# Index scores in small portions, two-bank ReLUs and sign-made masks in the token phase of a two-layer hybrid trunk

## The chip, the core and the metric

One core of one Trainium2 chip runs the whole program. The metric is the device time of one execution in microseconds (us): the median of three runs, and beside it one execution taken by the hardware profiler, from which all rows come.

## What is computed

Two layers over 1024 tokens of width 1024, float32. Every layer has one input projection, a sparse attention branch, a gated delta-rule branch, gates, and an output projection. The part that the change touches most is the lightning indexer, which picks 256 keys for each query:

```python
raw = jnp.einsum('bqhd,bsd->bqhs', qib, k_idx)                 # 8 heads of 64
iscore = jnp.einsum('bqhs,bqh->bqs', jax.nn.relu(raw), wb)
iscore = jnp.where(causal[None], iscore, -jnp.inf)
_, sel = lax.top_k(iscore, topk)                               # topk = 256, ties to the lower index
...
y_a = dsa_attention(q_a, k_a, v_a, q_i, k_i, w_i) * jax.nn.silu(z_a)
...
x = x + (gates[0] * y_a + gates[1] * y_b) @ w_out[layer]
```

The kernel doesn't gather keys: it makes a mask for every block of 128 queries whose row has more than 256 causal keys (blocks t = 2 to 7, with n = 128(t+1) keys, 384 to 1024), and attention adds the mask to its logits.

## The kernel before

Matrix products run as three products of rounded halves (high by high, high by low, low by high), so one product of 128 x 1024 by 1024 x 512 is 24 matmuls of 512 columns. PSUM has eight banks of 512 float32 columns for each partition. A layer goes through these stages:

- **make_h**: normalise x and transpose it (`tr` tiles, L289).
- **Token phase** (`token_phase`): the index projections; then three chunks of q, k and v, each over 8 token tiles (`proj_tokens`, L368, 24 matmuls a tile into an `acc` bank, emptied by ScalarE's copy `stage`, L415); then four gates, each of four `proj_feat` calls (L391, 24 matmuls; ScalarE's tanh `th`, L673, and VectorE's `gate`, L674, empty the bank). The weights are cast by ScalarE (`w_hi`, L150) and their rests made by VectorE (`w_lo`, L151).
- **Beside it** runs a generator, `self.beside`, first `index_scores`, then `select`. `index_scores` does, for each block and each pair of heads, 64-row matmuls for two heads side by side into `wide` banks (L554), a ReLU on ScalarE (L556), and on VectorE the weighted sum into `scores` (L561, L563). `select` finds the 256th largest score of every row by a search over 31 bits: in each step VectorE counts for blocks 5 and 7 (L589) and ScalarE does it by the sum of a Sign for blocks 4, 3, 2 and 6 (L607). Two such searches (`SEL_STAGES`) are interleaved. At its end VectorE makes the masks (L652 to L658: equal, a running count, two combinations, a product), and SyncE's queue stores them.
- **Feature phase** (gates of the other branch, convolutions, the delta rule), **attention** (L1131 logits, L1133 mask and row maximum, L1136 exponential, L1154 transposes, L1163 values) and the output projection.

The order of the work is that in which the program writes it: every engine takes its own instructions in that order. `tick`, called behind every token tile and every `proj_feat`, is what mixes the second stream in: it takes steps of `self.beside` until their costs come to `SHARE` = 4. A score step costs 2n/1024, a step of the search 1.5, and what the last step overshoots is forgotten. So the scores are written in bursts of up to 36 rows of matmul pairs between two token tiles, 11 bursts a layer; within a burst nothing else stands on PE between a pair of heads and the next. There are four one-bank `wide` tiles. For n over 512 a pair of heads is done in two equal halves of n (2 x 320, 2 x 384, 2 x 448, 2 x 512), with a ReLU for each half and head. Gates use the two `acc` banks alone. In layer 0 the token phase lies at 77 to 364 us of the span, in layer 1 at 1372 to 1654 us; the feature phase follows.

Of the kernel before, what the change touches and what calls it, by code (L numbers as in the profile page):

```python
# [58 lines left out]
SHARE, SEL_COST = 4.0, 1.5  # L59
# [19 lines left out]
STEP_PAIRS, STEP_CHUNKS = 6, 7  # L79

# [16 lines left out]
class Trunk:  # L97
    def __init__(self, ctx, tc, args):
# [10 lines left out]
        self.beside = None  # L109
# [185 lines left out]
    def tick(self):  # L295

        left = SHARE
        while left > 0 and self.beside is not None:
            cost = next(self.beside, None)
            if cost is None:  # L300
                self.beside = None
            else:
                left -= cost
# [50 lines left out]
    def proj_tokens(self, weights, act, evac, t0=0, tag=lambda t: "acc", then=None):  # L354
# [8 lines left out]
        for t, k in order:  # L363
# [3 lines left out]
            for i, (a, b) in enumerate(((act[0], 0), (act[0], 1), (act[1], 0))):  # L367
                nc.tensor.matmul(acc[t][:, :n], a[:, k, ts], ws[k][b][:, :n], start=k == 0 and i == 0,  # L368
                                 stop=k == KT - 1 and i == 2)
# [14 lines left out]
    def proj_feat(self, ws, half, act, evac, tag="acc"):  # L384

        hs = slice(half * 512, half * 512 + 512)
        acc = self.bank(tag)
        for k in range(KT):
            cs = slice((k % 4) * P, (k % 4 + 1) * P)
            for i, (a, b) in enumerate(((0, 0), (0, 1), (1, 0))):  # L390
# [7 lines left out]
        self.tick()  # L398


    def token_phase(self, l, ip, ht, first):
# [31 lines left out]
        with tc.tile_pool(name="tok", bufs=1) as p, self.banks(wide=(1, 4)):  # L433
            self.decays(l, p, raw)
            scores = {t: p.tile([P, (t + 1) * P], F32, name=f"scores{t}") for t in SEL}
            select = interleave([self.select(p, i, scores, *st) for i, st in enumerate(SEL_STAGES)])
            self.beside = itertools.chain(self.index_scores(l, p, raw, scores), select)
# [3 lines left out]
            for f in range(GATES[0]):  # L441
                self.gate_a(l, ht, f)
# [54 lines left out]
    def index_scores(self, l, p, raw, scores):  # L497
# [42 lines left out]
        later = queries(t0)  # L540
        for t in SEL:
# [3 lines left out]
            parts = 1 if n <= 512 else 2  # L545
            w = n // parts
            for i in range(IDXH // 2):
                rel = [p.tile([P, S], F32, name="relu", bufs=3) for _ in range(2)]
                for o in range(0, n, w):
                    ps = [self.bank("wide") for _ in range(2)]  # L550
                    for j, (a, b) in enumerate(((qh, kh), (qh, kl), (ql, kh))):
                        for half in range(2):
                            rows = slice(IDXD * half, IDXD * half + IDXD)
                            nc.tensor.matmul(ps[half][:, :w], a[rows, i], b[rows, o:o + w], start=j == 0, stop=j == 2)  # L554
                    for half in range(2):
                        nc.scalar.activation(rel[half][:, o:o + w], ps[half][:, :w], AF.Relu)  # L556
# [10 lines left out]
                yield 2 * n / S  # L567
# [3 lines left out]
    def select(self, p, which, scores, on_dve, on_act):  # L571
# [63 lines left out]
        for i in range(nb):  # L635
# [6 lines left out]
        for i in range(nb):  # L642
# [628 lines left out]
```

## Time and profile before

| what | value |
|---|---|
| median of 3 runs (lowest, highest) | 2610.4 us (2606.67, 2615.41) |
| the profiled execution's own time | 2613.37 us |
| its span, first to last instruction | 2611.6 us |
| mean granted TensorE clock over the span | 0.993 |
| PE busy | 2542.9 us, 97% |
| VectorE (DVE) busy | 1897.7 us, 73% |
| ScalarE (ACT) busy | 1344.3 us, 51% |
| GpSimd (POOL) busy | 160.0 us, 6% |

PE is the matmuls and PEld the weight loads that run under them. Matmuls are pipelined: a matmul of 512 columns is listed with about 0.4 us, while the next starts 0.23 us later. Idle time before an instruction is put down to the work that ended it (`<-` and an engine, a name and a line). PEclk is the granted clock as a share of full speed, so 0.50 is the lower of TensorE's two levels (1.2 instead of 2.4 GHz).

### The profile page before, as it was taken

Reading aid. Unit: us, or ns where it says so; the run is one execution under the profiler, and the core shown is the slowest. Engines: PE = TensorE matmul, PEld = TensorE weight load, DVE = VectorE, ACT = ScalarE, POOL = GpSimd, SP = SyncE. Lnnn points to the kernel's source line nnn. Section 1 sums busy time; section 2 is a strip of 40 time slices with the busy share of each in tenths; the row PEclk is TensorE's granted clock in tenths of the full one; section 3 lists DMA queues with packets and bytes.
Section 4 is the critical chain, followed back from the end, with each engine's and each line's share of the span. In section 5 each row is a group of like instructions: output and inputs, shape, how many; then the busy total and the mean of one; then the engine's idle time right before and its main releaser. Section 6 shows DMA issues by size and latency. Waiting matters only on the chain. (4 is left out here: it accounts for less than half of the span.)

```text
span 2611.6 us, 42034 instructions
## 1 busy us (share of the span) xinstructions
PE 2542.9 (97%) x14858; PEld 2110.7 (81%) x14858; DVE 1897.7 (73%) x5086; ACT 1344.3 (51%) x3107; POOL 160.0 (6%) x428
## 2 busy tenths in 40 slices
PE   7999999999999999999999999999999999999998
PEld 7777778888888888898796777878888888878986
DVE  7578977777887773797366779877777787647965
ACT  5559824444444333697245796333444444338952
POOL 0124000000000000000002340000000000000000
PEclk9999999999999999999999999999999999999999
DMA  4112333233333323430521232333223333324223
GB/s 126 50 57 80 91 92 81 54 67 71 72 66 75 70 56 95 147 101 30 164 59 42 65 98 76 91 75 76 50 65 76 68 70 74 101 78 130 85 79 136
DMA packets 296439, 211.35 MB, mean 81 GB/s; under 512 B 72290, under 2 KB 253604, under 8 KB 296228
## 3 DMA queue, kind: packets, MB, share of 16 engines
q1 hardware_dynamic: 290116, 188.73, 26.9%
q0 software_dynamic: 6112, 19.93, 3.2%
q8 instruction: 117, 1.92, 0.3%
q14 instruction: 94, 0.77, 0.1%
HBM read 162.19 MB, written 46.40 MB: 80 GB/s over the span
## 5 line engine op out<-in xcount | busy, mean ns | idle before, releaser
L391 PE MATMUL acc<-hi_t,w_hi 128*128 128x512 f32 x1240 | 505.1, 407 | 8.2 <-DVE gate L674 8.2
L391 PE MATMUL acc<-lo_t,w_hi 128*128 128x512 f32 x1240 | 504.2, 407 | 0.0
L391 PE MATMUL acc<-hi_t,w_lo 128*128 128x512 f32 x1240 | 500.5, 404 | 0.0
L150 ACT CAST w_hi<-w_raw 128x512 fp32r<-128x512 f32 (+1 forms) x336 | 201.4, 602 | 314.2 <-PE acc L391 161.4
L151 DVE TENSOR_TENSOR w_lo<-w_raw,w_hi 128x512 fp32r<-128x512 f32 (+1 forms) x336 | 223.9, 670 | 136.0 <-ACT w_hi L150 117.1
L368 PE MATMUL acc<-w_hi,hi_t 128*128 128x512 f32 (+1 forms) x768 | 285.9, 373 | 9.6 <-ACT stage L415 7.0
L368 PE MATMUL acc<-w_lo,hi_t 128*128 128x512 f32 (+1 forms) x768 | 284.3, 370 | 3.8 <-DVE w_lo L151 3.8
L368 PE MATMUL acc<-w_hi,lo_t 128*128 128x512 f32 (+1 forms) x768 | 283.2, 369 | 0.0
L391 PEld LDWEIGHTS acc<-hi_t,w_hi 128*128 128x128 f32 x1240 | 234.5, 189 | 56.8 <-DVE gate L674 10.0
L391 PEld LDWEIGHTS acc<-hi_t,w_lo 128*128 128x128 f32 x1240 | 234.6, 189 | 47.7
L391 PEld LDWEIGHTS acc<-lo_t,w_hi 128*128 128x128 f32 x1240 | 234.6, 189 | 45.7
L607 ACT ACTIVATE t_junk<-scores,t_bits 128x640 f16<-128x640 f32 x248 | 198.9, 802 | 35.2 <-DVE t_bits L599 26.0
L391 PE MATMUL more<-hi_t,w_hi 128*128 128x512 f32 x488 | 199.1, 408 | 0.0
L391 PE MATMUL more<-lo_t,w_hi 128*128 128x512 f32 x488 | 198.9, 408 | 0.0
L391 PE MATMUL more<-hi_t,w_lo 128*128 128x512 f32 x488 | 197.4, 405 | 0.0
L368 PEld LDWEIGHTS acc<-w_hi,hi_t 128*128 128x128 f32 x768 | 145.9, 190 | 40.4 <-ACT stage L415 8.7
L368 PEld LDWEIGHTS acc<-w_lo,hi_t 128*128 128x128 f32 x768 | 146.3, 190 | 29.8 <-DVE w_lo L151 7.7
L368 PEld LDWEIGHTS acc<-w_hi,lo_t 128*128 128x128 f32 x768 | 146.1, 190 | 21.9
L589 DVE TENSOR_SCALAR_CACHE_REDUCE t_junk<-scores,t_bits 128x1024 f16<-128x1024 f32 (+4 forms) x136 | 153.4, 1128 | 4.3
L563 DVE SCALAR_TENSOR_TENSOR scores<-relu,w_idx,scores 128x384 f32<-128x384 f32 (+5 forms) x84 | 80.7, 961 | 49.0 <-ACT relu L556 43.2
L963 DVE TENSOR_TENSOR xtmp<-wide,xc 128x60 f32<-128x60 f32 (+24 forms) x496 | 105.2, 212 | 14.2
L965 DVE TENSOR_TENSOR xc<-xc,xtmp 128x60 f32<-128x60 f32 (+24 forms) x496 | 105.2, 212 | 14.0
(347 smaller groups left out, 5380.1 us busy)
## 6 DMA issues: line engine op xcount, KB each, us to landing
w_raw<-in_w_in_dram SPq DMA_DIRECT2D x272, 256.0 KB
qs<-stage POOLq DMA_DIRECT2D x32, 256.0 KB, 2.4
ya_gate<-gate SPq DMA_DIRECT2D x32, 256.0 KB
H<-rows SPq DMA_DIRECT2D x16, 512.0 KB
wide<-hscr SPq DMA_DIRECT2D x64, 128.0 KB
yb<-gate SPq DMA_DIRECT2D x32, 256.0 KB
w_raw<-in_w_out_dram SPq DMA_DIRECT2D x32, 256.0 KB
qraw<-qs SPq DMA_DIRECT2D x32, 256.0 KB
```

Source lines behind the costliest of these rows:

```text
L150: self.nc.scalar.copy(hi, src)
L151: self.nc.vector.tensor_sub(lo, src, hi.bitcast(F32))
L368: nc.tensor.matmul(acc[t][:, :n], a[:, k, ts], ws[k][b][:, :n], start=k == 0 and i == 0, stop=k == KT - 1 and i == 2)
L391: mm = self.nc.tensor.matmul(acc, ws[k // 4][a][:, cs], act[b][:, k, hs], start=k == 0 and i == 0, stop=k == KT - 1 and i == 2)
L563: nc.vector.scalar_tensor_tensor(sc[:, :n], rel[half][:, :n], wc, sc[:, :n], op0=OP.mult, op1=OP.add)
L589: nc.vector.tensor_scalar(junk[:, :sc[i].shape[1]], sc[i], thr, 0.0, op0=op, op1=OP.add, accum_out=cnt[:, i:i + 1])
L607: nc.scalar.activation(junk[:, :n], sc[i], AF.Sign, bias=f(bits, i), scale=-1.0, accum_out=cnt[:, i:i + 1])
L963: nc.vector.tensor_mul(tmp[:, :n, j + 1:], ln[:, None, j, j + 1:].to_broadcast(shape), X[:, :n, j:j + 1].to_broadcast(shape))
L965: nc.vector.tensor_add(X[:, :n, j + 1:], X[:, :n, j + 1:], tmp[:, :n, j + 1:])
```

## The change

- `tick` takes the last matmul, is called every 12 matmuls (half a token tile or half a `proj_feat`), and adds `SHARE` = 2 to a credit that carries over, overshoot included. A score step costs 1.5 x 2n/1024, a search step 1.4. Steps are written right behind that matmul.
- `wide` is two tiles of two banks. A pair of heads fills columns 0 to 512 and then the rest (128, 256, 384 or 512) of its two tiles, and one ReLU for each head reads all n columns.
- `proj_feat` in the token phase's gates takes `acc` and `wide` in turn, so four tiles.
- The Sign's unused output has two buffers, not one.
- Masks: the counts before the last comparison run for ScalarE's blocks alone; the count of larger values goes; ScalarE makes one Sign for each block more (L665 in the new numbering), and VectorE makes the mask from it in six operations (equal to zero with its sum, running count, product, maximum, and a comparison times MASKED), written over the block's scores; the store goes to GpSimd's queue.
- Memory: the pool of the scores' work is closed when they are done; the feature phase's tiles are spread over four pools; the load of a first tile (`H`) of that phase is put behind the last gate's store, and a memset of `xf` goes from GpSimd to VectorE, later. In attention, row buffers (`pr`) fall from five to four.

```diff
-SHARE, SEL_COST = 4.0, 1.5
+SHARE, SCORE_COST, SEL_COST = 2.0, 1.5, 1.4
...
-    def tick(self):
-
-        left = SHARE
-        while left > 0 and self.beside is not None:
-            cost = next(self.beside, None)
...
+    def tick(self, mm):
+
+        if self.beside is None:
+            return
+        self.credit += SHARE
+        with self.tc.issue_after(mm.ins):
+            while self.credit > 0 and self.beside is not None:
+                cost = next(self.beside, None)
+                if cost is None:
+                    self.beside, self.credit = None, 0.0
+                else:
+                    self.credit -= cost
...
                 evac(t, acc.pop(t)[:, :n])
-                self.tick()
+            if k % 4 == 3:
+                self.tick(mm)
...
-        acc = self.bank(tag)
+        acc = self.bank(tag if isinstance(tag, str) else next(tag))[:, :512]
...
+            if k == KT // 2 - 1:
+                self.tick(mm)
...
-        with tc.tile_pool(name="tok", bufs=1) as p, self.banks(wide=(1, 4)):
+        with tc.tile_pool(name="sel", bufs=1) as p, self.banks(wide=(2, 2)), ExitStack() as scoring:
+            ps = scoring.enter_context(tc.tile_pool(name="tok", bufs=1))
...
-                self.gate_a(l, ht, f)
+                self.gate_a(l, ht, f, itertools.cycle(("acc", "wide")))
...
-            parts = 1 if n <= 512 else 2
-            w = n // parts
+            parts = [slice(o, min(o + 512, n)) for o in range(0, n, 512)]
...
-                for o in range(0, n, w):
-                    ps = [self.bank("wide") for _ in range(2)]
+                ps = [self.bank("wide") for _ in range(2)]
+                for cols in parts:
...
-                    for half in range(2):
-                        nc.scalar.activation(rel[half][:, o:o + w], ps[half][:, :w], AF.Relu)
+                for half in range(2):
+                    nc.scalar.activation(rel[half][:, :n], ps[half][:, :n], AF.Relu)
...
-                yield 2 * n / S
+                yield SCORE_COST * 2 * n / S
...
-                junk = p.tile([P, S], F16, name="t_junk2", bufs=1)
+                junk = p.tile([P, S], F16, name="t_sign", bufs=2)
...
-        for i in range(nb):
+
+        nc.vector.memset(cnt[:, :n_dve], 0.0)
+        for i in range(n_dve, nb):
             count(i, f(up, i), OP.is_ge)
...
-        for i in range(nb):
-            count(i, f(bits, i), OP.is_gt)
...
+        def signs(i):
+            sg[i] = p.tile([P, S], F16, name="t_sign", bufs=2)[:, :sc[i].shape[1]]
+            nc.scalar.activation(sg[i], sc[i], AF.Sign, bias=f(bits, i), scale=-1.0, accum_out=cnt[:, i:i + 1])
...
+            nc.vector.tensor_scalar(eq, sg[i], 0.0, 0.0, op0=OP.is_equal, op1=OP.add, accum_out=eqs[:, one])
...
+            nc.vector.tensor_tensor_scan(run, eq, eq, less[:, one], op0=OP.add, op1=OP.bypass)
+            nc.vector.tensor_mul(run, run, eq)
+            nc.vector.tensor_tensor(run, run, sg[i], op=OP.max)
...
+            msk = scores[t].bitcast(BF16)[:, :n]
+            nc.vector.tensor_scalar(msk, run, 0.0, MASKED, op0=OP.is_gt, op1=OP.mult)
+            nc.gpsimd.dma_start(out=self.masks[t], in_=msk)
...
-            r = self.rp.tile([P, T, P], F32, name="pr", bufs=5)
+            r = self.rp.tile([P, T, P], F32, name="pr", bufs=4)
```

The first place where the order of instructions moves is PE in the first q, k, v chunk of layer 0, where the scores of block 3 (n = 512) begin; `tr` is a transpose of the next block's queries, `acc` a token tile. Before, the end of one burst and the token tile behind it:

```order
L554 MATMUL wide<-k_hi,qi_hi 128x384 x2
L554 MATMUL wide<-k_lo,qi_hi 128x384 x2
L554 MATMUL wide<-k_hi,qi_lo 128x384 x2
L554 MATMUL wide<-k_hi,qi_hi 128x512 x2
L554 MATMUL wide<-k_lo,qi_hi 128x512 x2
L554 MATMUL wide<-k_hi,qi_lo 128x512 x2
L368 MATMUL acc<-w_hi,hi_t 128x512
L368 MATMUL acc<-w_lo,hi_t 128x512
L368 MATMUL acc<-w_hi,lo_t 128x512
```

The same block after the change, around half a token tile (L568 is the score matmul, L376 the token tile's):

```order
L568 MATMUL wide<-k_hi,qi_lo 128x512
...
L376 MATMUL acc<-w_hi,hi_t 128x512
L376 MATMUL acc<-w_lo,hi_t 128x512
L376 MATMUL acc<-w_hi,lo_t 128x512
...
L568 MATMUL wide<-k_hi,qi_hi 128x512 x2
L568 MATMUL wide<-k_lo,qi_hi 128x512 x2
L568 MATMUL wide<-k_hi,qi_lo 128x512 x2
L376 MATMUL acc<-w_hi,hi_t 128x512
```

A pair of heads used to stand right behind another; now 12 matmuls of a token tile stand between one pair of heads and the next nearly everywhere, and the scores reach to the 13th of the 24 token tiles, where they ended in the 8th. Counted over the order, the score matmuls of a layer stand on PE in 11 stretches before (with a token tile or transposes between two of them), and in 25 after.

The second place is ScalarE at the end of the token phase of layer 0 (`th` is a gate's tanh, `w_hi` a weight cast, `xp` the first copy of the feature phase). Before:

```order
L607 ACTIVATE t_junk_3441,t_cnt_2048<-scores_1075,t_bits_2051 128x896
L673 ACTIVATE th<-acc 128x512 x2
L150 CAST w_hi<-w_raw 128x512 x2
L673 ACTIVATE th<-acc 128x512
L150 CAST w_hi<-w_raw 128x512 x2
L673 ACTIVATE th<-acc 128x512 x3
...
L772 COPY xp_3957<-acc 128x512
```

After, where L665 is the Sign from which a mask is made and L700 a gate's tanh:

```order
L665 ACTIVATE t_sign,t_cnt_2149<-scores_1081,t_bits_2152 128x768
L665 ACTIVATE t_sign,t_cnt_2149<-scores_1080,t_bits_2152 128x640
L155 CAST w_hi<-w_raw 128x512
L700 ACTIVATE th<-acc 128x512
L665 ACTIVATE t_sign,t_cnt_2185<-scores_1083,t_bits_2188 128x1024
L700 ACTIVATE th<-wide 128x512
L665 ACTIVATE t_sign,t_cnt_2185<-scores_1082,t_bits_2188 128x896
L155 CAST w_hi<-w_raw 128x512
L665 ACTIVATE t_sign,t_cnt_2149<-scores_1079,t_bits_2152 128x512
...
L665 ACTIVATE t_sign,t_cnt_2149<-scores_1078,t_bits_2152 128x384
...
L806 COPY xp_3910<-acc 128x512
```

ScalarE's share of the selection used to end eight tanhs before the feature phase; six signs now stand among the last tanhs, and every second one of the gates' tanhs reads a `wide` tile. The third sign and those behind it write a buffer that VectorE must have read.

## Rows read from the trace of the kernel before

**Rows 1.** Stretches: busy of each engine (instructions), PEclk, share of DMA, GB/s.

```profile
77.00:175.00 98.00, 90.96 (x469) 66.31 (x468) 60.71 (x90) 54.18 (x117) 18.22 (x49) 0.93 0.15 47
175.00:318.00 143.00, 138.01 (x595) 111.08 (x594) 122.27 (x370) 129.62 (x293) 43.37 (x127) 1.00 0.30 88
318.00:358.00 40.00, 37.47 (x149) 29.64 (x148) 34.89 (x79) 6.49 (x11) 0.00 (x0) 0.91 0.22 67
358.00:1050.00 692.00, 690.69 (x4261) 569.02 (x4260) 496.92 (x1299) 277.36 (x718) 15.25 (x16) 1.00 0.32 72
1372.00:1649.00 277.00, 261.63 (x1209) 203.90 (x1208) 216.68 (x534) 190.24 (x420) 61.46 (x176) 0.98 0.24 72
```

**Rows 2.** Waits of PE: engine, line, releaser: us in total, times, longest.

```profile
PE wide L554 <- ACT relu L556: 11.7, 11, 3.8
PE acc L391 <- DVE gate L674: 8.2, 4, 2.5
PE acc L368 <- ACT stage L415: 7.0, 4, 2.2
```

**Rows 3.** Waits of the weight loads: the same columns.

```profile
PEld wide L554 <- ACT relu L556: 27.3, 53, 4.2
```

**Rows 4.** Timeline of PE in a burst, block 6: start, us, work.

```profile
136.11 0.37 PE L554 MATMUL wide<-k_hi,qi_lo 64*128 64x448 f32 x2
140.32 1.17 PE L554 MATMUL wide<-k_hi,qi_hi 64*128 64x448 f32 x2 [3.84 <-ACT relu L556]
```

**Rows 5.** Six stretches at half clock, as rows 1: one, and the sum.

```profile
139.90:146.70 6.80, 6.38 (x28) 4.89 (x28) 4.63 (x5) 5.54 (x13) 1.78 (x5) 0.50 0.11 41
sum 30.80, PE 28.51 PEld 22.18 DVE 22.25 ACT 14.13 POOL 4.24; mean PE 4.75 PEld 3.70 DVE 3.71 ACT 2.35 POOL 0.71
```

**Rows 6.** Timeline of PE into a burst of block 7 and out of it.

```profile
167.52 0.40 PE L368 MATMUL acc<-w_hi,lo_t 128*128 128x512 f32 x1
167.84 0.50 PE L554 MATMUL wide<-k_hi,qi_hi 64*128 64x512 f32 x2
168.18 0.40 PE L554 MATMUL wide<-k_lo,qi_hi 64*128 64x512 f32 x2
168.88 0.39 PE L554 MATMUL wide<-k_lo,qi_hi 64*128 64x512 f32 x2
169.11 0.39 PE L554 MATMUL wide<-k_hi,qi_lo 64*128 64x512 f32 x2
...
172.35 0.50 PE L368 MATMUL acc<-w_hi,hi_t 128*128 128x512 f32 x1
172.69 0.39 PE L368 MATMUL acc<-w_lo,hi_t 128*128 128x512 f32 x1
172.92 0.39 PE L368 MATMUL acc<-w_hi,lo_t 128*128 128x512 f32 x1
```

**Rows 7.** ScalarE's ReLUs by shape, 77:358: count, busy, mean ns, idle before.

```profile
L556 ACT ACTIVATE relu<-wide 128x512 f32<-128x512 f32 x24 | 12.9, 602 | 2.3 <-PE wide L554 1.1 <-DVE scores L563 0.9 <-DVE scores L561 0.2
L556 ACT ACTIVATE relu<-wide 128x320 f32<-128x320 f32 x16 | 6.1, 443 | 1.6 <-DVE scores L563 1.5
```

**Rows 8.** Timeline of ScalarE: two signs with one buffer; two squares (L1233) with two.

```profile
212.55 0.19 ACT L607 ACTIVATION_READ_ACCUMULATOR t_junk<-scores,t_bits 128x1 f32 x1
212.77 0.72 ACT L607 ACTIVATE t_junk<-scores,t_bits 128x512 f16<-128x512 f32 x1
...
2582.39 0.19 ACT L1233 ACTIVATION_READ_ACCUMULATOR sq_junk<-x 128x1 f32 x1
2582.48 0.62 ACT L1233 ACTIVATE sq_junk<-x 128x512 f32<-128x512 f32 x1
```

**Rows 9.** Timeline of VectorE in the mask tail of the first layer.

```profile
337.72 0.68 DVE L674 SCALAR_TENSOR_TENSOR gate<-th,acc 128x512 f32<-128x512 f32 x1
340.72 0.75 DVE L652 TENSOR_SCALAR t_junk<-scores,t_bits 128x1024 f16<-128x1024 f32 x1 [1.45 <-DMA mask<-t_junk]
```

**Rows 10.** VectorE's masking of logits in attention: count, busy, mean ns, idle before.

```profile
L1133 DVE CUSTOM_DVE_ANT_0 pr<-wide,mask 128x384 f32<-128x384 f32 (+3 forms) x96 | 56.9, 593 | 8.0 <-PE tr L1154 5.7 <-PE wide L1131 2.2
```

More of the change, by code (lines that the diff above doesn't have):

```diff
@@ L293, in make_h @@
         return ht
-    def tick(self):
-        left = SHARE
-        while left > 0 and self.beside is not None:
-            cost = next(self.beside, None)
[L300 to L303, printed above, removed]
+    def tick(self, mm):
[6 more added lines that the diff above has]
+                if cost is None:
+                    self.beside, self.credit = None, 0.0
+                else:
+                    self.credit -= cost
     def at(self, pos, step):
@@ L367, in proj_tokens @@
             for i, (a, b) in enumerate(((act[0], 0), (act[0], 1), (act[1], 0))):
-                nc.tensor.matmul(acc[t][:, :n], a[:, k, ts], ws[k][b][:, :n], start=k == 0 and i == 0,
-                                 stop=k == KT - 1 and i == 2)
+                mm = nc.tensor.matmul(acc[t][:, :n], a[:, k, ts], ws[k][b][:, :n], start=k == 0 and i == 0,
+                                      stop=k == KT - 1 and i == 2)
             if then and t == T - 1:
@@ L553, in index_scores @@
                             rows = slice(IDXD * half, IDXD * half + IDXD)
[L554 to L556 removed]
+                            nc.tensor.matmul(ps[half][:, cols], a[rows, i], b[rows, cols], start=j == 0, stop=j == 2)
+                for half in range(2):
+                    nc.scalar.activation(rel[half][:, :n], ps[half][:, :n], AF.Relu)
                 for half in range(2):
@@ L647, in select @@
+        signs(0)
         for i, t in enumerate(blocks):
             n = (t + 1) * P
-            thr = f(bits, i)
-            eq = p.tile([P, S], F16, name="t_junk", bufs=1)
-            run = p.tile([P, S], F16, name="t_run", bufs=1)
-            nc.vector.tensor_scalar(eq[:, :n], sc[i], thr, None, op0=OP.is_equal)
-            nc.vector.tensor_tensor_scan(run[:, :n], eq[:, :n], eq[:, :n], 0.0, op0=OP.add, op1=OP.bypass)
-            nc.vector.scalar_tensor_tensor(eq[:, :n], run[:, :n], rest[:, i:i + 1], eq[:, :n], op0=OP.is_gt,
-                                           op1=OP.mult)
@@ L656, in select @@
-            nc.vector.scalar_tensor_tensor(run[:, :n], sc[i], thr, eq[:, :n], op0=OP.is_lt, op1=OP.max)
-            msk = p.tile([P, S], BF16, name="t_junk", bufs=1)
-            nc.vector.tensor_scalar(msk[:, :n], run[:, :n], MASKED, None, op0=OP.mult)
-            nc.sync.dma_start(out=self.masks[t], in_=msk[:, :n])
+            if i + 1 < nb:
+                signs(i + 1)
+            eq = p.tile([P, S], F16, name="t_eq", bufs=1)[:, :n]
+            run = p.tile([P, S], F16, name="t_junk", bufs=1)[:, :n]
@@ L734, in plan_head, with zeros @@
         at(AT_CHUNKS, *[lambda: next(chunks, None)] * (3 * T - 1), gap=STEP_CHUNKS)
+    def zeros(self, a):
+        with self.tc.issue_after(self.behind):
+            self.nc.vector.memset(a, 0.0)
     def decays_load(self, p, hd):
         nc, h = self.nc, hd["h"]
-        E = hd["H"] = p.tile([P, T, P], F32, name="H", bufs=2)
-        with ExitStack() as ctx:
-            if h:
-                ctx.enter_context(self.tc.issue_after(self.back if h > 1 else self.taken))
+        E = hd["H"] = self.pd.tile([P, T, P], F32, name="H", bufs=2)
+        with self.tc.issue_after((self.stored, self.taken, self.back)[min(h, 2)]):
             nc.sync.dma_start(out=E, in_=ap(self.rows, h * P, [[0, P], [8 * P, T], [1, P]]))
@@ L1124, in probabilities @@
             nmax = BIG
-            row = self.rp.tile([P, S], F32, name="pr", bufs=5)[:, :n]
+            row = self.rp.tile([P, S], F32, name="pr", bufs=4)[:, :n]
             e = n if n <= 512 else n // 2
```

57 lines of the change are left out of this document (33 added, 24 removed).

## The prediction, made before the changed kernel was run

> **What bounds the kernel now.** I read the busy times of stretches first. In the feature phase PE is busy 690.69 of 692 us at full clock, so what the change does there can only cost. In the token phase PE is short of full: idle 7.0 of 98 us while the scores run, 5.0 of 143 in the search, 2.5 of 40 in the mask tail, and 15.4 of 277 in the second layer; the clock is at 0.93 and 0.91 in the first and third [rows 1]. ScalarE has 129.62 of 143 us of work in the search, VectorE 122.27: the stretch has little room on either [rows 1].
>
> Then the waits by what ended them, for both layers. PE's largest in this phase are for the ReLUs (11.7 us), the gates' banks (8.2) and the copies `stage` (7.0) [rows 2]. For the ReLUs the weight loads tell more: they wait 27.3 us, 53 times [rows 3], since a load stands at the head of the next pair and its matmul can't come before it. The longest of them shows why: a pair of heads ends at 136.11 us and the next begins at 140.32, behind a ReLU [rows 4]. Four one-bank tiles are two halves of one pair; nothing but scores stands behind them on PE, so any lag of ScalarE stops it.
>
> The clock comes with that. Six stretches of the two token phases, 30.8 us in all, run at half clock; the one at 139.90 follows on the wait just named [rows 5]. Half speed for 30.8 us is 15.4 us of matmul time lost.
>
> **The change, part by part** (both layers, against the profiled execution's 2613.4 us, which lies 3 us above the median of 2610.4; I give the result on the median's scale.)
>
> *Portions, two-bank tiles, one ReLU a head.* Between two pairs of heads PE now has 12 matmuls of 0.23 us [rows 6], 2.75 us. The ReLUs that free the tiles: by the two sizes seen, 443 ns for 320 columns and 602 for 512 [rows 7], a column costs 0.83 ns, so 1024 columns take about 1.03 us (an estimate), two heads 2.05 us. That lies within 2.75 us, and in this stretch ScalarE works 54.18 of 98 us [rows 1]. Only for block 2 (384 columns, cost 1.125 of a credit of 2) do two pairs sometimes follow each other, and a queue on ScalarE can still hold one up. I leave 2 us of the 27.3: **-25** (-27 to -18). Below -27.3 nothing is to be had here.
>
> *Clock.* With the long waits gone, four of the six slow stretches lose what stood ahead of them; the waits for the gates stand ahead of the others. I take **-12** of the 15.4 us (-15 to -4): what lets the clock fall may come back at the starts of the gates, where casts wait.
>
> *More changes between scores and token tiles.* The score matmuls stand in 25 stretches a layer instead of 11, so 28 more. Into one: the last token matmul at 167.52, the first score at 167.84, 0.32 instead of 0.23; the next score at 168.18, 0.34 instead of the 0.23 between 168.88 and 169.11. Out of one: 172.35 to 172.69 is 0.34, where 172.69 to 172.92 is 0.23 [rows 6]. So 0.09 + 0.11 + 0.11 and about 0.1 for the step from the last score to the first token matmul, the mirror of the way in: 0.41 us. 28 x 0.41 is **+11.5** (+8, if some changes stand beside transposes anyway, to +17 at 0.6 each). The Trainium skill, "TensorEngine Tiling (Array Packing)", section "Key Properties", says that changing the tiling mode, not just the tile, drains TensorE; score matmuls of 64 rows among those of 128 are such a change. By it the portions are paid for at every change. The trace agrees: 0.41 us at each.
>
> *Unequal parts.* For n = 640 the pieces are 512 and 128 instead of twice 320. From the rows of 448 and 512 a step goes with its columns; how short 128 may be no row shows. Between no loss and a step of 0.11 us instead of 0.06 for 24 pairs of matmuls: **+0.5** (0 to +1.5).
>
> *Gates in four tiles.* The wait is that for a bank whose `gate` stands on VectorE behind the mask work, as at 337.72 [rows 9]. Two more tiles give 2 x 5.6 us of slack (24 x 0.23), more than any of these waits (2.5 the longest) [rows 2]: **-8** (-8.2 to -3).
>
> *Signs and masks.* With one buffer, the next Sign starts 0.22 us behind the accumulator's read (212.55 to 212.77); where two buffers are to be had, 0.09 (2582.39 to 2582.48) [rows 8]. That saves some 0.13 us for two or three signs in each of 31 steps, about 10 us of ScalarE a layer. Search steps come 1.5/1.4, 7% closer, which takes about 9 of 130 back: ScalarE stays as loaded as it was, so the waits for `stage` (7.0) stay. On VectorE the counts of larger values go and with them the waits for a mask's store (1.45 us in one case) [rows 9]; both lie beside PE. New is that the third to sixth mask signs wait for a buffer that VectorE must have read, with `th` of the last gates and the first copy of the feature phase queued behind them on ScalarE. What would be late next is the last `acc` bank, wanted by the feature phase's second product: I allow 1 to 2 us a layer, **+3** in all (-5, if ScalarE gains more than it is asked for, to +19, below).
>
> *Casts.* The weight casts of a gate stand closer to its start, behind one or two signs: **+2** (0 to +10, eight starts of 1.2 us, two casts of 0.6).
>
> *Four row buffers in attention.* VectorE waits there 8.0 us in all, 5.7 of them for transposes, the readers of the rows [rows 10]; PE has no wait of note for it. **+2** (0 to +10).
>
> *Memory, `H`, `xf`, mask stores on another queue.* The feature phase shows no PE wait to remove (1.3 us idle in 692 [rows 1]); the cover is PE's own work, and without it a late `H` or `xf` would show as PE idle at the phase's start. **0** (-1 to +3). GpSimd has 43.37 of 143 us in the search and none in the tail [rows 1], so six stores there hold nothing up.
>
> Sum: -25 - 12 + 11.5 + 0.5 - 8 + 3 + 2 + 2 = **-26**. 2610.4 - 26 is **2584 us**.
>
> **Rivals.**
>
> *A: the waits and the clock go, and little is given back.* Changes at 8, casts and attention at nothing, all of the slow clock back: -27 - 15 + 8 - 8 = -42, 2568 us. For it: ScalarE's room while the scores run. Against: 0.41 us was the same in every clean change that I looked at.
>
> *B: the search becomes the bound.* The scores now end in the 13th token tile, not the 8th, and the search is squeezed between there and the end of the gates. If a second buffer does not shorten a Sign, 0.13 us for some 75 signs a layer, 10 us, comes out as waits for `stage` and `th`, twice: +19 instead of 0. -26 + 19 = -7 to -10, about 2602 us. For it: 129.62 of 143. Against: the search ran at that load before and cost PE 7.0 us.
>
> *C: the portions don't take the waits away.* ReLUs queue behind `stage` copies and casts on ScalarE as they did behind other ReLUs, so half the waits stay (-13), the clock with them (-4), and the changes are paid: -13 - 4 + 11.5 - 8 + 8 = about -5, 2605 us. It decides from a lag of 2.75 us of ScalarE at a portion. Against: 54.18 of 98.
>
> *D: slower, by attention.* 64 pairs of rows go through `pr` in both layers; with four buffers the logits of the next pair can wait until the transposes have read the last. At 0.4 us for each of 64, 26 us, the gain is gone, and from 0.55 on (35 us) the kernel is slower than before by over 0.3%; 0.6 gives 2584 + 38 = 2622 us. For it: VectorE already waits for transposes there [rows 10]. Against: those are 5.7 us over both layers, and PE shows none of it.
>
> **How the numbers follow.** The forecast (2572 to 2597) gets 0.58, A 0.12, B 0.14, C 0.09, D 0.07. A measurement of this kernel tells about 0.3% (8 us) from no change. Below 2602.6: the forecast, A, half of B and a quarter of C, and a little of D: 0.80. Within 8 us: the rest of B, C and some of D, 0.13. Slower: 0.07. The range from 2563 to 2604 leaves out D, half of C and the far end of B.
>
> **What would show it.** Waits of the weight loads for ReLUs near 2 us; the clock at 1.00 in both score stretches; no wait of `acc` for `gate`; the way in and out of a portion again 0.41 us, 25 times a layer; waits for `stage` still near 7 us. It would be wrong if ScalarE's lag showed at `stage`, `th` or the portions' ReLUs, if PE stood still at the start of the feature phase behind the last masks, or if attention grew longer with VectorE waiting there for transposes.

## The result, and the profile after

The changed kernel takes 2590.93 us (median of 4 runs, 2589.33 to 2592.86); the kernel before took 2612.9 us beside it (4 runs). The ratio is 0.9925 with a 95% interval of 0.9909 to 0.9941, so it is faster by 0.6 to 0.9%, some 20 us. The forecast was 2584 us, the range 2563 to 2604. The profiled spans are 2588.0 us now and 2611.6 us before, 23.6 us apart, at clocks of 0.998 and 0.993.

First the stretches of [rows 1], the same columns, of the changed kernel. The work has moved forward in them, so a stretch now holds more matmuls:

```profile
77.00:175.00 98.00, 96.99 (x518) 71.07 (x518) 57.61 (x94) 49.05 (x86) 29.45 (x75) 1.00 0.20 63
175.00:318.00 143.00, 137.26 (x593) 107.78 (x592) 123.06 (x358) 124.08 (x290) 33.77 (x103) 1.00 0.24 71
318.00:358.00 40.00, 39.91 (x171) 31.86 (x170) 38.79 (x107) 17.55 (x35) 2.70 (x5) 1.00 0.42 114
358.00:1050.00 692.00, 689.10 (x4265) 567.28 (x4265) 493.76 (x1299) 280.01 (x723) 15.90 (x16) 1.00 0.33 75
1372.00:1649.00 277.00, 266.10 (x1219) 205.70 (x1220) 214.18 (x536) 182.46 (x389) 66.78 (x177) 0.99 0.27 76
```

While the scores run, PE is busy 96.99 of 98 us (90.96 before) and does 518 matmuls there instead of 469; the clock is at 1.00 in both places where it was low. In the 40 us from 318 on (the gates' last product now ends near 347.7 us) PE and VectorE both have next to no idle time left. The feature phase has hardly changed: 2.9 us of idle in 692, 1.3 before.

What PE waits for in the token phase (total, times, longest), where [rows 2] had 11.7, 8.2 and 7.0 us:

```profile
PE more L400 <- ACT th L700: 5.2, 1, 5.2
PE acc L400 <- DVE w_lo L156: 3.5, 6, 1.3
PE acc L400 <- ACT w_hi L155: 3.1, 4, 1.2
...
PE acc L376 <- ACT stage L426: 2.8, 4, 0.8
```

and the weight loads at the score matmuls, where [rows 3] had 27.3 us:

```profile
PEld wide L568 <- issue: 13.7, 38, 0.4
...
PEld wide L568 <- ACT relu L570: 3.3, 10, 0.4
```

The 13.7 us marked `issue` wait for no other work: all 38 stand where PE comes from other work to the scores, and belong to the change from one to the other that is read below. The waits for ReLUs have fallen from 27.3 to 3.3 us, those for `gate` are gone, those for `stage` are 2.8 us instead of 7.0. Three are new: 5.2 us, once, for a tanh ahead of a `more` tile, and 3.5 and 3.1 us at the gates' products for the two halves of their weights.

A portion, from PE's timeline of the changed kernel:

```profile
165.42 0.40 PE L376 MATMUL acc<-w_hi,lo_t 128*128 128x512 f32 x1
165.75 0.49 PE L568 MATMUL wide<-k_hi,qi_hi 64*128 64x512 f32 x2
166.08 0.39 PE L568 MATMUL wide<-k_lo,qi_hi 64*128 64x512 f32 x2
...
167.01 0.40 PE L568 MATMUL wide<-k_hi,qi_lo 64*128 64x512 f32 x2
167.34 0.50 PE L376 MATMUL acc<-w_hi,hi_t 128*128 128x512 f32 x1
167.68 0.40 PE L376 MATMUL acc<-w_lo,hi_t 128*128 128x512 f32 x1
167.91 0.39 PE L376 MATMUL acc<-w_hi,lo_t 128*128 128x512 f32 x1
```

Into it 0.33 instead of 0.23 and once more 0.33, out of it 0.33 and 0.34: each is 0.10 or 0.11 over the plain step, four times, and so 0.41 us a portion, as in [rows 6].

The 5.2 us belong to the second layer alone. ScalarE there, from the last mask signs to the last tanh:

```profile
1622.01 0.72 ACT L665 ACTIVATE t_sign<-scores,t_bits 128x512 f16<-128x512 f32 x1 [2.74 <-DVE t_junk L682]
...
1623.24 0.59 ACT L700 ACTIVATE th<-acc 128x512 f32<-128x512 f32 x1
1627.96 0.61 ACT L665 ACTIVATE t_sign<-scores,t_bits 128x384 f16<-128x384 f32 x1 [4.13 <-DVE t_junk L682]
...
1628.57 1.12 ACT L155 CAST w_hi<-w_raw 128x512 fp32r<-128x512 f32 x2
1629.60 0.58 ACT L700 ACTIVATE th<-wide 128x512 f32<-128x512 f32 x1
```

and PE at the same time:

```profile
1624.61 0.40 PE L400 MATMUL acc<-lo_t,w_hi 128*128 128x512 f32 x1
1630.24 0.80 PE L400 MATMUL more<-hi_t,w_hi 128*128 128x512 f32 x1 [5.24 <-ACT th L700]
```

The gates' last tanh (`th<-wide`) could have run from about 1624 us on. Ahead of it in ScalarE's order stands the Sign of the last block, and that waits 4.13 us until VectorE has read the sign of another block out of the buffer (L682). PE's first product of the feature phase needs a `more` tile, which lies where the gates' `wide` tile lay. PE does five matmuls of the next product, in an `acc` tile, and then stands still for 5.24 us. Its next matmuls run at the low clock:

```profile
1628.60:1635.40 6.80, 5.16 (x12) 4.10 (x13) 6.70 (x17) 1.59 (x4) 1.08 (x2) 0.50 0.53 140
```

That is the one half-clock stretch left in the token phases: 6.8 us where there were 30.8 [rows 5].

### The profile page after: what moved, and what is told of

Read it like the earlier page. It is cut to its first block, busy times and chain, and to the rows that moved or that the text cites. A ratio compares the mean times of both kernels' runs of the same rounds, so it can differ in the third digit from the quotient of the medians.

```text
span 2588.0 us, 41984 instructions
## 1 busy us (share of the span) xinstructions
PE 2530.8 (98%) x14858; PEld 2096.6 (81%) x14858; DVE 1879.1 (73%) x5092; ACT 1335.6 (52%) x3067; POOL 169.1 (7%) x438
## 5 line engine op out<-in xcount | busy, mean ns | idle before, releaser
L400 PE MATMUL acc<-hi_t,w_hi 128*128 128x512 f32 x1112 | 453.0, 407 | 3.3 <-ACT w_hi L155 3.1
L400 PE MATMUL acc<-hi_t,w_lo 128*128 128x512 f32 x1112 | 449.0, 404 | 3.5 <-DVE w_lo L156 3.5
L400 PE MATMUL acc<-lo_t,w_hi 128*128 128x512 f32 x1112 | 451.8, 406 | 0.0
L376 PE MATMUL acc<-w_hi,hi_t 128*128 128x512 f32 (+1 forms) x768 | 287.4, 375 | 5.4 <-ACT stage L426 2.8
L376 PE MATMUL acc<-w_lo,hi_t 128*128 128x512 f32 (+1 forms) x768 | 283.3, 369 | 2.6 <-DVE w_lo L156 2.5
L376 PE MATMUL acc<-w_hi,lo_t 128*128 128x512 f32 (+1 forms) x768 | 282.5, 368 | 0.0
L400 PEld LDWEIGHTS acc<-hi_t,w_lo 128*128 128x128 f32 x1112 | 209.5, 188 | 47.3 <-DVE w_lo L156 6.1
L400 PEld LDWEIGHTS acc<-hi_t,w_hi 128*128 128x128 f32 x1112 | 209.4, 188 | 46.9 <-ACT w_hi L155 5.8
L400 PEld LDWEIGHTS acc<-lo_t,w_hi 128*128 128x128 f32 x1112 | 209.5, 188 | 39.1
L621 ACT ACTIVATE t_sign<-scores,t_bits 128x640 f16<-128x640 f32 x248 | 195.9, 794 | 16.2 <-DVE t_bits L613 13.3
L376 PEld LDWEIGHTS acc<-w_hi,hi_t 128*128 128x128 f32 x768 | 145.0, 189 | 38.3 <-issue 7.6
L376 PEld LDWEIGHTS acc<-w_lo,hi_t 128*128 128x128 f32 x768 | 145.3, 189 | 26.1 <-DVE w_lo L156 4.8
L376 PEld LDWEIGHTS acc<-w_hi,lo_t 128*128 128x128 f32 x768 | 145.2, 189 | 23.5 <-issue 1.0
L603 DVE TENSOR_SCALAR_CACHE_REDUCE t_junk<-scores,t_bits 128x768 f16<-128x768 f32 x124 | 142.1, 1146 | 4.2
```

Of the source, the lines that this page charges most:

```text
L376: mm = nc.tensor.matmul(acc[t][:, :n], a[:, k, ts], ws[k][b][:, :n], start=k == 0 and i == 0, stop=k == KT - 1 and i == 2)
L400: mm = self.nc.tensor.matmul(acc, ws[k // 4][a][:, cs], act[b][:, k, hs], start=k == 0 and i == 0, stop=k == KT - 1 and i == 2)
L603: nc.vector.tensor_scalar(junk[:, :sc[i].shape[1]], sc[i], thr, 0.0, op0=op, op1=OP.add, accum_out=cnt[:, i:i + 1])
L621: nc.scalar.activation(junk[:, :n], sc[i], AF.Sign, bias=f(bits, i), scale=-1.0, accum_out=cnt[:, i:i + 1])
```

## The experiments

Each ran beside the kernel before on the same chip; ratios are to it, with 95% intervals. The expectations stand as they were written ahead of the runs. An interval is some 3 to 5 us to each side, so two experiments that lie less than about 5 us apart are not told apart by their times alone; there the waits have to decide. The question behind them: the forecast's sum held, but which of its terms did, and what holds the rest of the change up?

**1. The portions alone, on the kernel before.** `tick`, its calls, the costs and the credit as in the change, and nothing else of it:

```diff
-SHARE, SEL_COST = 4.0, 1.5
+SHARE, SCORE_COST, SEL_COST = 2.0, 1.5, 1.4
...
-                yield 2 * n / S
+                yield SCORE_COST * 2 * n / S
```

> The kernel before with the new order of the scores alone (half-tile steps, carried credit, one pair of heads a portion); still four one-bank tiles, halves of n with a ReLU each, gates in two banks, old masks, one sign buffer. If the portions are what takes the ReLU waits away: the weight loads' wait for ReLUs falls from 27.3 to under 6 us, the clock stays full while the scores run, and the time is about 2612 - 18 = 2594 us, with the gates' waits (8 us) still there. If the two-bank tiles are what does it: over 15 us of ReLU waits stay, the added changes cost 10 us, and the time is 2605 to 2615.

2645.27 us, ratio 1.0118 (1.0098 to 1.0139): slower by 1.2%. Neither theory said so. What the first says of the ReLU waits held, by the weight loads:

```profile
PEld wide L561 <- ACT relu L563: 1.8, 6, 0.4
```

The first layer's gates begin at 250.3 us of the span instead of 267.5, so 17 us were gained up to there. All of it and more is lost behind the gates; PE's longest waits of the whole run are these:

```profile
PE more L395 <- ACT kf L780: 31.6, 1, 31.6
PE acc L395 <- ACT kf L780: 30.6, 1, 30.6
```

31 us in each layer, for the first convolution's copy `kf`. ScalarE shows what that waited for, and VectorE, in the mask tail, what made it late:

```profile
387.63 1.27 ACT L780 ACTIVATE kf<-acc,feat 128x512 f32<-128x512 f32 x2 [29.23 <-DMA mask<-t_junk]
```

```profile
353.07 0.75 DVE L659 TENSOR_SCALAR t_junk<-scores,t_bits 128x1024 f16<-128x1024 f32 x1 [3.50 <-DMA mask<-t_junk]
```

The convolution's tile lies over the masks' buffer, so it waits for the last mask's store. The masks all go through that one buffer, so each also waits for the store before it, 3.5 us for the 1024-wide block's. In the kernel before, ScalarE waited for the same store at the same place, but only for 2.8 us, and PE did not wait at all:

```profile
378.83 1.27 ACT L773 ACTIVATE kf<-acc,feat 128x512 f32<-128x512 f32 x2 [2.80 <-DMA mask<-t_junk]
```

Two things have moved. The last mask's store of the first layer is issued at 385.9 us instead of 377.1, 9 us later, and the feature phase's first copy `xp` starts at 346.7 instead of 369.6, 23 us sooner. So the larger part of the 31 us is PE's own gain, which it can't keep: it comes to the feature phase before the masks are done.

**2. The masks over the scores, on top of experiment 1.**

```diff
-            msk = p.tile([P, S], BF16, name="t_junk", bufs=1)
+            msk = scores[t].bitcast(BF16)
```

> Portions alone on the kernel before, as in the run that was slower, but with the masks written over the scores instead of into the one buffer that each store must leave first. There VectorE waited some 13 us a layer for stores and PE 31 us for the first convolution, whose tile lay over that buffer. If the stores' single buffer makes the tail late: VectorE's waits for stores go, PE's wait falls from 31 to 10 to 20 us a layer, about 2610 to 2620 us. If the place of the first convolution's tile over the tail's memory is all: the wait stays over 25 us, 2635 to 2645.

2613.03 us, ratio 0.9996 (0.9987 to 1.0006). The first reading holds: PE's wait is 18.1 us in one layer and 17.4 in the other instead of 31.6 and 30.6, and the time is 32 us shorter, of which these waits are 26.7. The last store is issued at 372.3 us, still 26 us behind the first `xp` copy (39 us in experiment 1, 7.5 in the kernel before). What is left of the waits is that store, now out of the scores, where the first convolution's tile lies now:

```profile
ACT kf L780 <- DMA mask<-scores: 16.1, 1, 16.1
```

**3. The memory of before, in the changed kernel.** The four pools of the feature phase are the two of before again:

```diff
-        with tc.tile_pool(name="early", bufs=1) as pe, tc.tile_pool(name="decays", bufs=1) as pd, \
-                tc.tile_pool(name="late", bufs=1) as pl, tc.tile_pool(name="feat", bufs=1) as p, \
+        with tc.tile_pool(name="early", bufs=1) as pe, tc.tile_pool(name="feat", bufs=1) as p, \
```

> The changed kernel with the feature phase's tiles in the two pools of before (early, feat), so that the first convolution's tiles lie over what the mask tail still uses. Portions alone, with the old memory and the old masks, made PE wait 31 us in each layer for the first convolution's copy, which waited for the last mask's store. If the split memory is what avoids this: PE waits at the first products of the feature phase, 10 to 25 us a layer (the tail is shorter here than in that run), 2610 to 2640. If the shorter mask tail alone avoids it: within 4 us of 2591.

2590.72 us, ratio 0.9911 (0.9898 to 0.9925), the same as the changed kernel. ScalarE waits for a store here too,

```profile
ACT kf L806 <- DMA mask<-scores: 7.9, 1, 7.9
```

but PE shows none of it: the last store is issued 6.4 us behind the first `xp` copy, as in the changed kernel (6.4) and nearly as in the kernel before (7.5). So the split memory buys slack, some 8 us in the first layer and 0.6 in the second, and no time in this kernel. The second reading holds for the time. That it is the masks' shorter tail which is enough is argued, not shown: this kernel differs from experiment 2 in the other parts of the change too.

**4. The masks of before, in the changed kernel** (still over the scores, still stored by GpSimd's queue).

```diff
+        for i in range(nb):
+            count(i, f(bits, i), OP.is_gt)
...
+            nc.vector.tensor_scalar(eq[:, :n], sc[i], thr, None, op0=OP.is_equal)
```

> The changed kernel with the masks of before (counts of larger values, equal, running count, two combinations, product, all on VectorE), still written over the scores and stored by GpSimd's queue. If the sign-made masks matter by VectorE's time: the tail starts 6 to 7 us later behind the added counts and ends later, PE waits for `gate` or the first convolution, 2595 to 2605. If they cost by their queue on ScalarE: the second layer's 5.2 us wait for a tanh goes, and the time is 2583 to 2588.

2597.33 us, ratio 0.9933 (0.9920 to 0.9945), 6.6 us over experiment 3 on the same chip, which takes the changed kernel's time. (Beside the changed kernel's own ratio, 0.9925, the intervals overlap.) The first reading holds: VectorE is late for the first convolution, and PE waits for it at the transposes behind it,

```profile
PE tr L813 <- DVE kf L804: 6.8, 2, 5.5
```

while the wait for a tanh is 2.4 us instead of 5.2.

**5. The old calls and costs of the scores, in the changed kernel.**

```diff
-SHARE, SCORE_COST, SEL_COST = 2.0, 1.5, 1.4
+SHARE, SCORE_COST, SEL_COST = 4.0, 1.0, 1.5
...
-        self.credit += SHARE
+        self.credit = SHARE
```

> The changed kernel with the old order of the scores (one call a token tile, a share of 4, score cost 2n/1024, overshoot forgiven, search step 1.5); two-bank tiles, gates in four tiles and the new masks stay. If the portions carry the gain: ReLU waits of the weight loads of over 15 us come back, the clock falls in the score stretches, the score stretches are 11 a layer again, and the time is 2600 to 2612. If the two-bank tiles carry it: waits under 6 us and 2585 to 2592, better by the changes saved.

2616.21 us, ratio 1.0012 (1.0001 to 1.0022): without the portions the change is worth nothing. The old order did not come back with the old calls, though: counted over the trace, the scores of a layer stand in 25 stretches here too, not in 11 as expected, but mostly with one to five token matmuls between two pairs of heads instead of 12. So the changes between scores and token tiles are still paid, and the run tells what the distance between the pairs is worth. The ReLU waits are back, and new ones of the gates' weights with them:

```profile
PEld wide L564 <- ACT relu L566: 18.3, 38, 2.8
```

```profile
PE acc L399 <- ACT w_hi L155: 13.0, 2, 6.5
```

These and the slow clock are part of the 25 us lost against the changed kernel: the clock is at its lower level for 34 us of the token phases, 20.4 of them around the gates' starts, waits included.

**6. Gates in two banks, in the changed kernel.**

```diff
-                self.gate_a(l, ht, f, itertools.cycle(("acc", "wide")))
+                self.gate_a(l, ht, f)
```

> The changed kernel with the token phase's gates in the two acc banks alone. If four tiles are worth what was predicted: waits of PE for gate or th at the gates come back, 8 us and up to 6 us of slow clock behind them, while the second layer's 5.2 us wait of the first product of the feature phase goes: 2591 to 2600. If the wait only moves from the gates to the feature phase's first product: 2585 to 2591.

2591.16 us, ratio 0.9919 (0.9903 to 0.9936), no different. The tanh's wait in the second layer goes, and two others take its place, at the gates and (once) at a tile that VectorE's mask work holds. This one stands in the first layer, at the feature phase's first product (353.37 us): its `acc` bank is emptied by a `gate` that runs on VectorE only at 352.63 us, behind mask work. No wait for `gate` comes back between the gates' own products:

```profile
PE acc L400 <- DVE w_lo L156: 8.2, 6, 1.8
PE acc L400 <- DVE t_less L678: 5.5, 1, 5.5
```

**7. `acc` tiles first in each feature phase.**

```diff
             self.pe, self.pd = pe, pd
+            self.turn = 0
```

> The changed kernel, the rotation of the banks set to its start at the head of each feature phase, so that the second layer's feature phase begins with two acc tiles, as the first layer's does, and not with the more tile that lies where the gates' wide tiles lay. If that tile is what waits for a tanh queued behind the last mask sign: the 5.2 us wait and the half-clock stretch of 6.8 us behind it go, 5.2 + 3.4 = 8.6 us, 2582 us. If ScalarE's lag stops PE whichever bank comes first: the wait shows at an acc tile, and the time stays within 3 us of 2591.

2584.66 us, ratio 0.9893 (0.9876 to 0.9910), 6 us better than the change. The first reading holds in the main: the wait for the tanh and the half-clock stretch behind it are gone, 1.3 us of it shows at the second `acc` tile, and the waits at the gates' starts stay, with a stretch of 3.4 us at half clock that is new there:

```profile
PE acc L400 <- ACT w_hi L155: 4.8, 6, 1.2
...
PE acc L400 <- DVE t_less L678: 1.3, 1, 1.3
```

**8. The last mask sign in its own buffer.**

```diff
-            sg[i] = p.tile([P, S], F16, name="t_sign", bufs=2)[:, :sc[i].shape[1]]
+            n = sc[i].shape[1]
+            sg[i] = p.tile([P, 384], F16, name="m_small", bufs=1) if n == 384 else \
+                p.tile([P, S], F16, name="t_sign", bufs=2)[:, :n]
```

> The changed kernel, the last mask sign (block 2, 384 columns) written to a small buffer of its own, so that it no longer waits for VectorE to have read the sign of block 6; banks as in the changed kernel. If the tanh that holds the `more` tile in the second layer is late because it stands behind that sign: the 5.2 us wait and the slow clock behind it go, 2582 to 2586 us, with ScalarE's 4.1 us wait of that sign gone. If the tanh is late because of VectorE's or ScalarE's load as such: the wait stays over 3 us, 2588 to 2593.

2588.45 us, ratio 0.9903 (0.9888 to 0.9918). The sign no longer waits, but the tanh still runs 3.7 us after the gates' last product has ended (1625.1 to 1628.86; 1623.7 to 1629.60 in the changed kernel), since the next thing ahead of it in ScalarE's order waits in turn:

```profile
1624.74 0.59 ACT L702 ACTIVATE th<-acc 128x512 f32<-128x512 f32 x1
1625.23 0.61 ACT L155 CAST w_hi<-w_raw 128x512 fp32r<-128x512 f32 x1
1628.34 0.62 ACT L155 CAST w_hi<-w_raw 128x512 fp32r<-128x512 f32 x1 [2.50 <-DMA w_raw<-in_w_in_dram]
1628.86 0.59 ACT L702 ACTIVATE th<-wide 128x512 f32<-128x512 f32 x1
```

It is a cast that waits 2.5 us for its weights. PE still waits 3.1 us. So the cause is the queue ahead of the tanh, and the sign only its longest member. By its marks (a wait over 3 us, 2588 to 2593) the second theory holds, narrowly.

**9. One buffer for the counting signs.**

```diff
-                junk = p.tile([P, S], F16, name="t_sign", bufs=2)
+                junk = p.tile([P, S], F16, name="t_eq", bufs=1)
```

> The changed kernel, the counting Signs' unused output back in one buffer. If the second buffer is what lowered the waits for `stage` from 7.0 to 2.8 us and keeps the search within its time: the step from a sign's read to the next sign is 0.22 us again instead of 0.09, waits for `stage` and at the gates grow by 5 to 20 us, 2596 to 2610. If ScalarE has room in the changed order: within 3 us of 2591.

2590.26 us, ratio 0.9909 (0.9895 to 0.9922): no loss, the second reading. (The one buffer is `t_eq`, which VectorE's masks use too; no counting Sign waits for that.) Signs do follow each other at 0.22 us after a read again, but casts now stand between single signs in ScalarE's order:

```profile
271.81 0.61 ACT L155 CAST w_hi<-w_raw 128x512 fp32r<-128x512 f32 x1
272.31 0.62 ACT L621 ACTIVATE t_eq<-scores,t_bits 128x384 f16<-128x384 f32 x1
...
272.93 0.61 ACT L155 CAST w_hi<-w_raw 128x512 fp32r<-128x512 f32 x1
```

In the changed kernel they stand together, two of them here behind the start of the gate that needs them (its first matmul is at 276.80 us):

```profile
277.36 1.13 ACT L155 CAST w_hi<-w_raw 128x512 fp32r<-128x512 f32 x2
```

The waits of the gates' weights are gone, and the first convolution waits instead:

```profile
PE tr L825 <- DVE kf L816: 9.2, 2, 6.2
PE acc L376 <- ACT stage L426: 3.7, 4, 1.0
...
PE more L400 <- ACT th L700: 2.8, 1, 2.8
```

**10. Gate weights a gate ahead.** The next gate's weights are asked for behind the first of a gate's four products:

```diff
                 self.proj_feat(ws[i], half, ht, evac, tag)
+                if half == 0 and i == 0 and after is not None:
+                    self.ready = [self.feat_weights(w, c + after * P) for c in (C_ZA, C_GA)]
```

> The changed kernel, with the weights of the next token-phase gate loaded, cast and split from the first product of the gate before it on, so that their casts stand on ScalarE ahead of the gate's start. If the waits at the gates' starts come from casts that stand too late in ScalarE's order: PE's waits for w_hi and w_lo at L400 (6.6 us) go to under 2, no half-clock stretch in the gates, and the time falls by 6 to 9 us to 2582 to 2585 us; the second layer's wait for a tanh stays. If ScalarE is simply too loaded to cast in time: the same wait shows at the gates under another name, 2588 to 2592.

2586.41 us, ratio 0.9903 (0.9888 to 0.9918), between the two readings' times. The waits for weights at the gates fall from 6.6 to 2.3 us (1.6 for `w_hi`, 0.7 for `w_lo`), no stretch at half clock is left at the gates, and some of it comes back behind them: 3.0 us for the first convolution, and at the tanh, where the changed kernel waits 5.2 us,

```profile
PE more L400 <- ACT th L701: 6.4, 1, 6.4
```

**11. All mends together**, 7, 8 and 10, and score parts in equal halves, one in each bank of a tile.

> All the mends together on the changed kernel: feature phases begin with acc tiles, gate weights a gate ahead, the last mask sign in its own small buffer, and score parts in equal halves again (one in each bank of the tile, one ReLU over both). If the losses add up as read from the trace (8.6 us for the second layer's stall, some 8 for the gates' starts, 1 for the parts): 2574 to 2578 us. If they share one cause, ScalarE's lag at the end of the search: 2580 to 2585, with the waits at the last masks.

2580.65 us, ratio 0.9874 (0.9859 to 0.9889), the fastest: 33.6 us under the kernel before, 10 under the change. It lies at the edge of the second reading. What is left of the waits is one for the first convolution, behind VectorE's masks, in each layer:

```profile
PE tr L834 <- DVE kf L825: 6.8, 2, 4.0
```

**12. The same, with the search sooner** (`SEL_COST` 1.3).

> The kernel with all the mends together, which took 2580.7 us, with a search step's cost of 1.3 instead of 1.4, so that the masks are written some 10 us of PE's time sooner. What is left there is 6.8 us of PE's waits for the first convolution, which VectorE does behind the last masks. If the masks' start is set by where the steps stand in the program: that wait goes and the time falls by 5 to 10 us, to 2571 to 2576. If ScalarE's and VectorE's load sets the pace of the search: the tail starts no sooner, and waits for `stage` or `gate` grow instead, 2579 to 2590.

2583.62 us, ratio 0.9898 (0.9880 to 0.9917), not better. Each reading has half: the wait for the convolution goes, as the first says, the time is the second's, and 9.2 us stand at the first gate of each layer instead, whose weights ScalarE casts late:

```profile
PE acc L400 <- ACT w_hi L155: 9.2, 2, 4.6
```

## Why the prediction held, step by step

**ReLU waits: right, and at their size.** -25 was written; the waits fell by 24.0 us. Experiments 1 and 5 put it on the portions and not on the two-bank tiles: 1.8 us of waits with one-bank tiles and portions, 18.3 us with two-bank tiles and one to five matmuls between most pairs. The estimate of a 1024-column ReLU, 1.03 us, was right too:

```profile
L570 ACT ACTIVATE relu<-wide 128x1024 f32<-128x1024 f32 x8 | 7.8, 1024 | 8.2 <-PE wide L568 8.2
```

**Clock: right.** -12 was written. 30.8 us at half clock became 6.8, and PE was busy in 28.51 and 5.16 us of them; half of the difference, 11.7 us, came back. (The 15.4 us of the prediction count PE as busy throughout; half of 28.51 is 14.3.) The one stretch left in the token phases stands behind the wait for the tanh, and it is gone with that wait in experiment 7, which has a new one of 3.4 us behind a shorter wait (last section).

**Changes between scores and token tiles: right.** 0.41 us each was read ahead and is 0.41 us again. By the rule named in the prediction (the Trainium skill, "TensorEngine Tiling (Array Packing)", "Key Properties": a change of the tiling mode drains TensorE), each portion pays this; the rows of the portion above agree. A change of product alone costs nothing: from a `more` tile's last matmul (364.60 us) to the next `acc` tile's first (364.83) PE takes the plain 0.23 us.

**Unequal parts: not weighed by a run of its own.** In the changed kernel the steps between pairs of 128 columns are 0.06 and 0.11 us (117.60, 117.66, 117.77 us), as the term allowed.

**Gates in four tiles: the size came, not by the tiles alone.** The 8.2 us for `gate` are gone. But with two banks (experiment 6) only one wait of 5.5 us comes back, behind the gates, and the time is the same; and the portions alone, with two banks, left 2.5 us for `gate` (experiment 1). What four tiles save in the first layer, the tanh's queue takes in the second. That -8 fits -8.2 is luck in part.

**Casts: mis-sized.** +2 was written, 6.6 us are there (3.5 and 3.1). It follows from a term that the prediction took for a gain of ScalarE's alone. The second sign buffer closes the gap between signs (0.09 us instead of 0.22, below), and in the order that is made with it the casts no longer stand between signs. Experiment 9 takes it back, and they do again. The other runs agree with this, those with weights asked for ahead aside: the ones with one buffer for the counting Signs (before, experiments 1, 2 and 9) have no waits for weights at the gates' products, and the changed kernel and experiments 3 to 8 have them. So the order on ScalarE isn't simply that in which the program writes the steps, as the text ahead of the prediction has it; the number of buffers moves it.

```profile
274.43 0.19 ACT L621 ACTIVATION_READ_ACCUMULATOR t_sign<-scores,t_bits 128x1 f32 x1
274.52 0.60 ACT L621 ACTIVATE t_sign<-scores,t_bits 128x384 f16<-128x384 f32 x1
```

**Signs and masks: mechanism right, the size low, one place missed.** +3 was written. The queue behind the mask signs is what the prediction described, but the tile that it holds is the second layer's `more` tile: 5.2 us, and 2.6 of slow clock (half of the 5.16 us worked at the low level), 7.8 us. With `acc` first (experiment 7) 6.3 us came back. The waits for `stage`, which were to stay at 7.0, fell to 2.8. The second sign buffer is not the reason, since they are 3.7 us without it (experiment 9); portions alone have 3.1 (experiment 1), and experiment 5, without them, 3.4, so more than one part of the change does it. That the new masks pay on VectorE (the prediction had them beside PE) is shown by experiment 4: some 6 us.

**Attention: nothing.** +2 was written; PE waits no longer there than before. VectorE waits more for transposes, 8.7 us where [rows 10] had 5.7, and that stays beside PE:

```profile
L1167 DVE CUSTOM_DVE_ANT_0 pr<-wide,mask 128x384 f32<-128x384 f32 (+3 forms) x96 | 56.8, 594 | 9.0 <-PE tr L1188 8.7
```

**Memory: 0 was right, but its cover was not weighed.** The prediction named PE's own work as what hides it. In the trace of before, ScalarE waits 2.8 us for a mask's store at the first convolution (experiment 1); PE doesn't, and the prediction passes it over. It says that the masks are only just done there: with the last store 39 and 26 us behind the first copy instead of 7.5, experiments 1 and 2 lose 31 and 18 us a layer. In the changed kernel the distance is 6.4 us and nothing is lost, with either memory (experiment 3).

Worked out from the two profiles: -24.0 (ReLU) - 11.7 (clock) + 11.5 (changes, 28 at the 0.41 us read) - 8.2 (gates) + 6.6 (casts) + 5.2 (tanh) - 4.2 (`stage`) = -24.8 us, against 23.6 us between the spans. Small differences elsewhere are left out, such as a half-clock stretch of 3.4 us at 1314 us that only the profile before has, outside the token phases.

The forecast's -26 is near this partly by luck. Casts cost 4.6 us more than written and the tanh 2.2 more than the whole +3, while `stage` gave 4.2 us that were not counted and attention took none of its 2.

Of the rivals, A fails by the 0.41 us a change, C by the 3.3 us of ReLU waits, D by attention. B's condition did not come, since the second buffer does close the gap between signs, but something like it is there, in small: what is left after each mend stands at the end of the search, on ScalarE's or VectorE's queue. That no single theory of the last microseconds settled it is how experiments 8, 10 and 12 read: the same 3 to 9 us move from one place to another. Which of ScalarE and VectorE is first short there was not told apart.

## What to carry to other kernels

A burst of short products that ScalarE empties should be cut into pieces, with enough matmuls between two of them to cover the emptying; here 2.75 us of matmuls cover 2.05 us of ReLUs, and with one to five matmuls between most pairs nothing was gained. Before the work of one engine is moved ahead of another's, look at what waits off the critical path for the other's end: a 2.8 us wait on ScalarE, hidden, told that the masks were only just in time, and portions alone, which bring PE there 23 us sooner, lost 33 us by it. An instruction that waits on another engine holds everything behind it on its own queue, so a tile released by that queue should not be the first that the next stage asks for.

## What was not expected of the hardware

A short wait can cost more by the clock than by itself, or nothing. At one place, a gate's start in the first layer, PE waits 1.28 us in experiment 7, and 3.4 us at the lower level follow (279.3 to 282.8 us), which is 1.7 us lost; experiments 3, 4 and 8 have the same there. In the changed kernel, which differs from experiment 7 only from the feature phase on, the wait is 1.29 us (to 279.29 us), and the clock stays at the upper level.

A long wait costs little more behind it than a middling one. Behind 5.2 us in the changed kernel PE does 5.2 us of work at the lower level. In experiment 1 PE stands still from 357.8 to 388.4 us in the first layer, and the clock is at the lower level from 360.5 to 391.2 us, so 2.8 us of work ran slowly behind that wait; in the second layer it is 6.1 us behind 31.6. Behind the 17.4 and 18.1 us of experiment 2 it is 5.7 and 5.1 us.
